# A two-layer hybrid decoder step on one core: sample transposes later, first-layer keys laid out by token tile, scans that start from the neighbouring block's column

## The chip, the cores and the metric

One core of a Trainium2 chip runs the whole step as one program. The metric is the device time of an execution in microseconds (us); the median of three runs stands for the kernel, and one further execution is profiled. The engines are PE (matrix products), PEld (its weight loads), DVE (vector), ACT (activations), POOL (GpSimd) and SP (which issues the DMAs here).

## The reference

One step over a prompt of 1024 tokens and 8 sample groups of 8 tokens (64 sample rows), width 1024, float32. Layer 0 is gated linear attention (GLA, 4 heads, key width 128, value width 256), layer 1 is stick-breaking attention (16 heads of 64). Both end in `x + (mixer(norm(x)) * silu(gate)) @ w_out`. Cut to what matters:

```python
# layer 0, per chunk of 64 tokens and per head; b is the running sum of the log decay
qd = qc * exp(b);  kd = kc * exp(-b)
att = where(causal, qd @ kd.T, 0)
o = qd @ s + att @ vc
s_new = s * exp(b_last)[:, None] + (kc * exp(b_last - b)).T @ vc

# layer 1, per head: key s is read by query t iff s < t
z = q @ k.T * dh ** -0.5 + bias
log_1mb = where(valid, log_sigmoid(-z), 0)
rest = cumsum(log_1mb, axis=3, reverse=True)
a = exp(where(valid, z + rest, -inf))
o = a @ v
```

The samples do the same, with a GLA state of their own (8 states per head) and, in layer 1, 256 keys and values from a paged cache before their own 8. Outputs are the new activations, the GLA states, and the keys and values of layer 1.

## The kernel before

Tokens are worked in tiles of 128: t = 0 to 7 are the prompt (NP = 8), t = 8 the 64 sample rows. Wide products are float32 split in a high and a low part (`whi`, `wlo`, `h0`, `h1`), three products for one: `dense` (L293) gives token rows, `dense_t` (L315) gives transposed columns, both into a bank `acc` of PSUM. PSUM is a pool with two banks per name (`acc`, `z`, `tr`, `o`): a third tile of a name waits until the first one's readers are done.

A time line written by hand sets the order of **PE**'s instructions: `at(time, function)` puts a step at a time whose unit is one dense tile, and steps are emitted in that order. The order of all other engines' queues is made by a scheduler that runs over the whole program; each engine then takes its own queue strictly in order and waits on semaphores.

**Layer 0.** For each head, three column stretches of queries and keys (`CH`) come from `dense_t`; `q_out` (L491) and `k_out` (L500) write five products into one tile `g` of 1536 columns: queries by exp(b) at 0, keys by exp(-b) at 384, keys by the decay to the tile's end at 768, and two half-tile products at 1152 and 1344. `gla_att` (L539) then makes a tile's scores `pat` with three products: all keys against the first 64 queries (L546), the first 64 keys against the last 64 queries (L547), the last 64 keys against the last 64 queries (L548), the last two into upper and lower partitions. Per head the sample states are read by `sample_out` (L610, product L615, two groups of states per call) and updated by `sample_state` (L620, product L625 into `z`, then DVE L628); both are called for b = 0, 2, 4, 6, at S_OUT + 0.05 b and S_STATE + 0.08 b after the head's last tile.

**Layer 1.** Heads go in 8 pairs. A pair's columns (384 per token tile) are made tile by tile, `columns(t)`, with gates after each second tile. For each tile DVE sums squares (`qk_sums`, L796), POOL raises them to the power -0.5 (L798) and DVE scales (`qk_scale`, L804), which frees the bank `acc`. Transposes on PE (L823) follow: `qk_p` for two prompt tiles, `qk_s` for the samples. The last column step of a pair is the samples' (t = NP), ending at time e; `qk_scale` of it is placed at e + C_SC (0.6), `qk_s` at e + C_T (0.9). The next pair's columns start at e.

Attention works in units: one head, 128 x 2 queries against 256 keys. `logits` (L875) puts scores in `z`, ACT makes `om` (1 - sigmoid) and `A` (L878, L879), POOL masks both when the unit is on the diagonal (L884). `stick` (L887) makes the running product from right to left with a DVE scan per half (L900) into `run`, 257 columns wide; column 256 holds what the block behind gives: 1 by a POOL memset (L894) on the diagonal, else a DVE copy of that block's column 0 (L896). The scan's first value is read from that column, and `A` is multiplied by `run` one column to the right (L905 diagonal, L908 else). `turn` (L910) transposes `A` on PE (L924), `weigh` (L936) multiplies by the values.

```python
    C_SC, C_T = 0.6, 0.9
    at(e + C_T, qk_s, st, p)
    at(z0 + L_STICK, stick, u, pair, m, c, j)
    at(z0 + L_TURN, turn, u, m, c)
```

Of the kernel before, what the change touches and what calls it, by code (L numbers as in the profile page):

```python
# [24 lines left out]
GH, DK, DV = 4, 128, 256  # L25
# [51 lines left out]
def tile_hybrid_decoder(ctx, tc, x_prompt, x_sample, state_gla, cache_k, cache_v, page_table,  # L77
# [3 lines left out]
    nc = tc.nc  # L81
# [24 lines left out]

    C_SC, C_T = 0.6, 0.9
    UNIT0, PACE, L_STICK, L_TURN, L_AV = 1.45, 0.42, 0.26, 0.8, 1.3
# [307 lines left out]
    for t in range(NP + 1):  # L416
        st = {}
# [73 lines left out]
    def q_out(st, h, c):  # L491
        n, nt = CH[c][1], (3, 3, 2)[c]

        g = st["g"] = sb("l0", "g", [128, 1536], F32, 3)
        nc.vector.scalar_tensor_tensor(g[:, :n], st["q"][:, :n], DK ** -0.5, st["e1"][:, :n],
                                       op0=OP.mult, op1=OP.mult)
        nc.vector.scalar_tensor_tensor(v3(g[:, 1152:], nt, 64), v3(st["q"], nt)[:, :, 64:], DK ** -0.5,
                                       st["e3"][:, :nt], op0=OP.mult, op1=OP.mult)

    def k_out(st, h, c):  # L500
        n, nt = CH[c][1], (3, 3, 2)[c]
        g = st["g"]
        nc.vector.tensor_mul(g[:, 384:384 + n], st["k"][:, :n], st["e2"][:, :n])
        nc.vector.tensor_mul(g[:, 768:768 + n], st["k"][:, :n], st["e4"][:, :n])
        nc.vector.tensor_mul(v3(g[:, 1344:], nt, 64), v3(st["k"], nt)[:, :, :64], st["e5"][:, :nt])

# [32 lines left out]
    def gla_att(st, t):  # L539
        g, o = st["g"], (t % 3) * 128  # L540
        pat = bank("z")
        att = st["att"] = sb("l0", "att", [128, 128], F32, 1)
        tr = psum.tile([128, 4, 128], F32, name="tr")
        if t < NP:
            o2 = 1344 + (t % 3) * 64
            nc.tensor.matmul(pat[:, :64], g[:, 384 + o:512 + o], g[:, o:o + 64], start=True, stop=True)  # L546
            nc.tensor.matmul(pat[:64, 64:128], g[:, o2:o2 + 64], g[:, o + 64:o + 128], start=True, stop=True)  # L547
            nc.tensor.matmul(pat[64:, 64:128], g[:, 448 + o:512 + o], g[:, o + 64:o + 128], start=True, stop=True)  # L548
            nc.vector.tensor_mul(att, pat[:, :128], C0["cmask"])
            split_att(st, 128)  # L550
            if t > 0:

                qh, ql = st["qs"] = [sb("l0", x, [128, 128], F32R, 1) for x in ("qh", "ql")]
                for x, y in ((slice(0, 64), o), (slice(64, 128), 1152 + (t % 3) * 64)):
                    nc.scalar.activation(qh[:, x], g[:, y:y + 64], AF.Copy)
                    nc.vector.tensor_sub(ql[:, x], g[:, y:y + 64], qh[:, x])
            nc.tensor.transpose(tr[:, 0, :], g[:, 768 + o:896 + o], ident)
            kh, kl = st["ks"] = [sb("l0", x, [128, 128], F32R, 1) for x in ("kh", "kl")]
            nc.scalar.activation(kh, tr[:, 0, :], AF.Copy)
            nc.vector.tensor_sub(kl, tr[:, 0, :], kh)  # L560
        else:
            nc.tensor.matmul(pat[:64, :64], g[:, 384 + o:448 + o], g[:, o:o + 64], start=True, stop=True)
            nc.vector.tensor_mul(att[:64, :64], pat[:64, :64], C0["smask"].rearrange("p b t -> p (b t)"))
            split_att(st, 64)
            nc.vector.tensor_copy(C0["qdm"].rearrange("p g (b s) -> p g b s", s=40)[:, :, :, :TS],
                                  g[:, o:o + 64].rearrange("p (g b s) -> p g b s", g=2, s=TS))
            nc.tensor.transpose(tr[:64, 0, :], g[:, 768 + o:832 + o], ident)

            kp = sb("l0", "kh", [128, 128], F32R, 1)
            nc.scalar.activation(kp[:64], tr[:64, 0, :], AF.Copy)  # L570
            nc.vector.tensor_sub(kp[64:], tr[:64, 0, :], kp[:64])
            ksm = st["ksm"] = sb("mid", "x4", [128, D + 1], F32R, 3)
            nc.vector.tensor_mul(ksm[:, :D].rearrange("p (b s) -> p b s", b=NB),
                                 kp[:, None].to_broadcast([128, NB, 128]),
                                 C0["blk2"][:, :, None].to_broadcast([128, NB, 128]))
# [80 lines left out]
    for h in range(GH):  # L656
# [24 lines left out]
        for t in range(NP + 1):  # L681
# [205 lines left out]
    def stick(u, pair, m, c, j):  # L887
# [93 lines left out]
    for p in range(PAIRS):  # L981
# [4 lines left out]
        def columns(t, i, span):  # L986
# [252 lines left out]
```

## Time and profile before

| | |
|---|---|
| three runs | 1405.91, 1409.91, 1410.98 us; median 1409.91 |
| profiled execution | 1409.71 us; its span 1407.7 us |
| granted TensorE clock, mean | 0.981 |
| PE / PEld busy | 1298.7 us (92%) / 1149.4 us (82%) |
| DVE, ACT, POOL busy | 1036.2 (74%), 710.7 (50%), 564.0 (40%) us |
| chain that ended last | PE 58%, DVE 20%, issue 8%, ACT 6%, POOL 5%, DMA 3% |
| DMA | 115.82 MB, mean 82 GB/s |

Layer 0 fills the span from 0 to about 445 us (some 95 us a head), its output product goes to about 538, layer 1's eight pairs follow at about 89 us each to 1251, and the samples' attention with the last output product ends it. A share of the span is an average over these; what a change is worth is read in its own stage. A wait is put down to the instruction that released it last. The view by stretch has, per row: the stretch, its length, the busy time of PE, PEld, DVE, ACT and POOL (x instructions) in it, the granted TensorE clock (1.00 is 2.4 GHz, 0.50 is 1.2 GHz), the DMA share and GB/s.

### The profile page before, as it was taken

What the parts mean: (1) busy time and instruction counts of PE and PEld (TensorE: products, weight loads), DVE (VectorE), ACT (ScalarE), POOL (GpSimd) and SP (SyncE); (2) the same over time, 40 slices, a digit from 0 to 9 for tenths busy, and PEclk for the clock granted to TensorE, in tenths of its full rate; (3) what the DMA queues carried; (4) which work ended last, traced back from release to release, by engine and by line L of the source; (5) the groups of instructions that cost most, each with busy time, mean ns of one, the idle gap of its engine ahead of it and who ended that gap; (6) DMA issues with size and microseconds to landing.
All of it is one profiled execution on the core that took longest, in us unless ns stands there. A gap on an engine that the chain in (4) does not pass through costs nothing.

```text
span 1407.7 us, 23743 instructions
## 1 busy us (share of the span) xinstructions
PE 1298.7 (92%) x8089; PEld 1149.4 (82%) x8089; DVE 1036.2 (74%) x2139; ACT 710.7 (50%) x1640; POOL 564.0 (40%) x1005
## 2 busy tenths in 40 slices
PE   6999999999999998989889898998998989889998
PEld 5788887888877788879889898897987988877666
DVE  7848648558464357688888888888888898897453
ACT  6445145253451034566756666566665666663221
POOL 6223314224131206464545645546464564542000
PEclk9999999999999999999999999999999999999999
DMA  7311402304336433020110201102012022133772
GB/s 190 90 31 42 133 15 70 106 22 120 102 115 223 128 105 108 19 76 22 56 41 20 77 17 48 53 24 75 18 37 63 22 80 62 41 113 116 266 254 90
DMA packets 118458, 115.82 MB, mean 82 GB/s; under 512 B 11002, under 2 KB 97922, under 8 KB 118338
## 3 DMA queue, kind: packets, MB, share of 16 engines
q1 hardware_dynamic: 118338, 114.31, 26.5%
q8 instruction: 64, 1.05, 0.3%
q14 instruction: 56, 0.46, 0.1%
HBM read 83.61 MB, written 30.67 MB: 81 GB/s over the span
## 4 chain that ended last, share of the span: by engine, by line
PE 58%; DVE 20%; issue 8%; ACT 6%; POOL 5%; DMA 3%; SPq 0%; POOLq 0%; DVEq 0%; ACTq 0%
PE acc L293 34%; PE acc L315 7%; DVE run L900 5%; PE z L875 3%; PE tr L924 3%; PE o L936 2%; DVE A L908 2%; ACT qh L847 2%; DVE A L905 1%; POOL rs L798 1%; PE o L537 1%; DVE whi L221 1%; DVE aT L927 1%; PE tr L277 1%; POOL wlo L222 1%
## 5 line engine op out<-in xcount | busy, mean ns | idle before, releaser
L293 PE MATMUL acc<-whi,h 128*128 128x512 f32 (+1 forms) x1728 | 548.0, 380 | 14.1 <-DVE qk L804 13.5
L293 PEld LDWEIGHTS acc<-whi,h 128*128 128x128 f32 x1728 | 320.3, 193 | 45.6 <-ACT gt L860 12.3
L293 PE MATMUL acc<-wlo,h 128*128 128x512 f32 (+1 forms) x864 | 326.7, 378 | 3.9 <-DVE wlo L222 2.5
L900 DVE TENSOR_TENSOR_SCAN run<-om,run 128x256 f32<-128x256 f32 (+1 forms) x320 | 231.5, 762 | 6.7 <-POOL om L884 4.2
L315 PE MATMUL acc<-h,whi 128*128 128x256 f32 (+5 forms) x832 | 191.8, 315 | 5.2 <-ACT h L282 2.9
L222 POOL TENSOR_TENSOR wlo<-wr,whi 128x512 fp32r<-128x512 f32 x98 | 139.4, 1427 | 140.9 <-DVE whi L221 111.6
L293 PEld LDWEIGHTS acc<-wlo,h 128*128 128x128 f32 x864 | 165.9, 192 | 23.2 <-DVE wlo L222 3.2
L926 ACT ACTIVATE aT<-tr 128x512 fp32r<-128x512 f32 (+1 forms) x160 | 88.9, 555 | 122.4 <-PE tr L924 117.3
L315 PEld LDWEIGHTS acc<-h,whi 128*128 128x128 f32 (+2 forms) x832 | 139.2, 186 | 10.1 <-issue 5.0
L878 ACT ACTIVATE om<-z,bias 128x512 f32<-128x512 f32 (+1 forms) x160 | 103.1, 645 | 51.2 <-PE z L875 32.7
L293 PE MATMUL acc<-w,h 128*128 128x384 f32 (+1 forms) x480 | 126.7, 375 | 1.8 <-DVE qk L804 1.8
L798 POOL TENSOR_TENSOR rs<-ms,half_exp 128x4 f32<-128x4 f32 (+1 forms) x72 | 95.3, 1323 | 79.6 <-DVE ms L796 79.3
L927 DVE TENSOR_TENSOR aT<-tr,aT 128x512 fp32r<-128x512 f32 (+1 forms) x160 | 100.8, 630 | 33.1 <-ACT aT L926 31.0
L315 PE MATMUL acc<-h,wlo 128*128 128x256 f32 (+2 forms) x392 | 122.9, 314 | 0.7 <-POOL wlo L222 0.7
L924 PE MATMUL tr<-ident,A 128*128 128x128 f32 x576 | 93.4, 282 | 28.2 <-DVE kc L853 21.2
L924 PEld LDWEIGHTS tr<-ident,A 128*128 128x128 f32 x576 | 72.0, 145 | 42.8 <-issue 24.5
L936 PE MATMUL o<-aT,v 128*128 128x256 f32 x640 | 102.3, 282 | 0.0
L879 ACT ACTIVATE A<-z,bias 128x512 f32<-128x512 f32 (+1 forms) x160 | 102.2, 639 | 0.0
L936 PEld LDWEIGHTS o<-aT,v 128*128 128x128 f32 x640 | 95.8, 190 | 0.7
L875 PE MATMUL z<-kc,qh 128*128 128x256 f32 x320 | 85.6, 289 | 7.3 <-DVE kc L852 7.3
L293 PEld LDWEIGHTS acc<-w,h 128*128 128x128 f32 x480 | 85.3, 195 | 8.5 <-issue 2.5
L875 PE MATMUL z<-kc,ql 128*128 128x256 f32 x320 | 84.6, 286 | 0.0
(274 smaller groups left out, 2444.0 us busy)
## 6 DMA issues: line engine op xcount, KB each, us to landing
wr<-in_w_in_b_dram SPq DMA_DIRECT2D x64, 256.0 KB, 3.0
wr<-in_w_in_a_dram SPq DMA_DIRECT2D x32, 256.0 KB, 2.7
kp<-in_cache_k_dram SPq DMA_DIRECT2D x16, 512.0 KB, 5.3
vp<-in_cache_v_dram SPq DMA_DIRECT2D x16, 512.0 KB, 4.7
o_d<-og SPq DMA_DIRECT2D x60, 128.0 KB, 1.8
x<-in_x_prompt_dram SPq DMA_DIRECT2D x8, 512.0 KB, 5.0
wr<-in_w_in_a_dram SPq DMA_DIRECT2D x32, 128.0 KB, 3.0
n<-in_state_gla_dram SPq DMA_DIRECT2D x8, 512.0 KB, 3.9
```

Source lines behind the costliest of these rows:

```text
L222: engine.tensor_sub(e.lo[:, :m], raw[:, :m], e.hi[:, :m])
L293: nc.tensor.matmul(st["ps"][:x.shape[1], :n], x, (w[k].hi if part == 0 else w[k].lo)[:, :n], start=first, stop=last)
L315: nc.tensor.matmul(st[key][:x.shape[1], :n], x, y, start=first, stop=last)
L798: nc.gpsimd.tensor_tensor(st["rs"][:n], ms[:n], half_exp[:n], op=OP.pow)
L875: nc.tensor.matmul(out, lhs, rhs, start=x == 0, stop=x == len(mm) - 1)
L878: nc.scalar.activation(u["om"][:, v0:], z[:, v0:], AF.Sigmoid, scale=-1.0, bias=K1["bias"][:, 1, hd:hd + 1])
L879: nc.scalar.activation(u["A"][:, v0:], z[:, v0:], AF.Sigmoid, bias=K1["bias"][:, 0, hd:hd + 1])
L900: nc.vector.tensor_tensor_scan(run[:, a, n - 1::-1], rev, rev, run[:, a, n:n + 1], op0=OP.mult, op1=OP.bypass)
L924: nc.tensor.transpose(tr[:, x], u["A"][:, col:col + 128], ident)
L926: nc.scalar.activation(hi[:, v0:], tr[:, v0:], AF.Copy)
L927: nc.vector.tensor_sub(lo[:, v0:], tr[:, v0:], hi[:, v0:])
L936: nc.tensor.matmul(q["po"][:, j], vs, part[:, x * 256:(x + 1) * 256], start=first and n == 0, stop=last and n == 3)
```

## The change

Four parts. (1) `qk_s` moves from e + 0.9 to e + 2.1 (C_TS). (2) The keys by exp(-b) and by the half-tile decay are written interleaved by token tile, 64 columns each: first half by exp(-b), first half by the half-tile decay, second half by exp(-b). The last 64 queries then meet 128 neighbouring columns in one product, so that a tile has two products of 128 x 64 where it had three; the quarter that is not causal is masked as before. The samples' keys get a small multiply of their own. (3) All `sample_out` calls of a head stand at one time, and `sample_state` calls stand 0.13 b apart instead of 0.08 b. (4) A scan takes its first value straight from the block behind (`before[:, a, 0:1]`, or 1.0 on the diagonal); the copy of that column, which the multiply still needs, goes from DVE to POOL.

```diff
-    C_SC, C_T = 0.6, 0.9
+    C_SC, C_T, C_TS = 0.6, 0.9, 2.1
...
     def k_out(st, h, c):
-        nc.vector.tensor_mul(g[:, 384:384 + n], st["k"][:, :n], st["e2"][:, :n])
-        nc.vector.tensor_mul(g[:, 768:768 + n], st["k"][:, :n], st["e4"][:, :n])
-        nc.vector.tensor_mul(v3(g[:, 1344:], nt, 64), v3(st["k"], nt)[:, :, :64], st["e5"][:, :nt])
+        def halves(x):
+            return x[:, :nt * 128].rearrange("p (c a s) -> p c a s", a=2, s=64)
+        by_tile = g[:, 384:384 + nt * 192].rearrange("p (c a s) -> p c a s", a=3, s=64)
+        nc.vector.tensor_mul(by_tile[:, :, 0::2], halves(st["k"]), halves(st["e2"]))
+        if c == 2:
+            nc.vector.tensor_mul(g[:, 768:832], st["k"][:, 256:320], st["e2"][:, 256:320])
+        nc.vector.tensor_mul(g[:, 960:960 + n], st["k"][:, :n], st["e4"][:, :n])
+        nc.vector.tensor_mul(by_tile[:, :, 1], v3(st["k"], nt)[:, :, :64], st["e5"][:, :nt])
...
     def gla_att(st, t):
-            nc.tensor.matmul(pat[:, :64], g[:, 384 + o:512 + o], g[:, o:o + 64], start=True, stop=True)
-            nc.tensor.matmul(pat[:64, 64:128], g[:, o2:o2 + 64], g[:, o + 64:o + 128], start=True, stop=True)
-            nc.tensor.matmul(pat[64:, 64:128], g[:, 448 + o:512 + o], g[:, o + 64:o + 128], start=True, stop=True)
+            nc.tensor.matmul(pat[:, :64], g[:, kt:kt + 128], g[:, o:o + 64], start=True, stop=True)
+            nc.tensor.matmul(pat[:, 64:128], g[:, kt + 64:kt + 192], g[:, o + 64:o + 128], start=True, stop=True)
...
-                    at(i + S_OUT + 0.05 * b, sample_out, st, b)
-                    at(i + S_STATE + 0.08 * b, sample_state, st, h, b)
+                    at(i + S_OUT + 0.2, sample_out, st, b)
+                    at(i + S_STATE + 0.13 * b, sample_state, st, h, b)
...
-    at(i + 2.2, closed, "l0")
+    at(i + 2.5, closed, "l0")
...
     def stick(u, pair, m, c, j):
-            nc.vector.tensor_copy(run[:, :, 256:], before[:, :, 0:1])
+            nc.gpsimd.tensor_copy(run[:, :, 256:], before[:, :, 0:1])
         for a in range(2):
             n = ends[a]
+            init = 1.0 if diag else before[:, a, 0:1]
-            nc.vector.tensor_tensor_scan(run[:, a, n - 1::-1], rev, rev, run[:, a, n:n + 1],
+            nc.vector.tensor_tensor_scan(run[:, a, n - 1::-1], rev, rev, init,
                                          op0=OP.mult, op1=OP.bypass)
...
-                at(e + C_T, qk_s, st, p)
+                at(e + C_TS, qk_s, st, p)
```

How this moves the queues, in three places. The line numbers of the changed kernel differ by some lines, a scan is printed as SCALAR_TENSOR_TENSOR, and [waits X_49] names the engines whose semaphores an instruction waits for.

**PE, between the second pair and the third.** Before, the sample transposes (L823, `qk 128x64`) stand inside the next pair's second column step:

```order
L936 MATMUL o<-aT_7949,v_7404 128x256 [waits Activation_49,Pool_49]
L936 MATMUL o<-aT_7950,v_7404 128x256 [waits DVE_49,Pool_49]
L936 MATMUL o<-aT_7949,v_7404 128x256
L936 MATMUL o<-aT_7950,v_7404 128x256
L293 MATMUL acc<-wlo,h_80 128x384
L823 MATMUL tr<-ident,qk 128x64 [waits DVE_49,PE_49]
L823 MATMUL tr<-ident,qk 128x64
L293 MATMUL acc<-whi,h_81 128x384
L293 MATMUL acc<-whi,h_80 128x384
L293 MATMUL acc<-wlo,h_80 128x384
L293 MATMUL acc<-whi,h_81 128x384
```

In the change (there L829) they stand behind that pair's first gates, some 65 rows of PE's queue later:

```order
L315 MATMUL acc<-h_80,w_7799 128x256
L293 MATMUL acc<-whi,h_80 128x384 [waits DVE_49,PE_49,Activation_49]
L293 MATMUL acc<-wlo,h_80 128x384
L932 MATMUL tr<-ident,A 128x128 x4
L293 MATMUL acc<-whi,h_81 128x384
L829 MATMUL tr<-ident,qk 128x64 [waits PE_49]
L829 MATMUL tr<-ident,qk 128x64
L881 MATMUL z<-kc,qh 128x256
L881 MATMUL z<-kc,ql_5787 128x256
```

The wait for DVE that stood on them is gone from them; the products behind them no longer follow them.

**DVE, the first two units of the third pair.** Before, the copy (L896) stands between a unit's multiplies (L905) and the next unit's scans (L900), and the scan waits for it:

```order
L900 SCALAR_TENSOR_TENSOR run<-om,run 128x128 [waits Pool_49]
L900 SCALAR_TENSOR_TENSOR run<-om,run 128x256
L905 TENSOR_TENSOR A<-A,run 128x128 [waits DVE_49,Pool_49]
L905 TENSOR_TENSOR A<-A,run 128x256 [waits DVE_49]
L896 COPY run<-run 128x2
L796 TENSOR_REDUCE ms_8095<-sq 128x4 [waits Activation_49]
L900 SCALAR_TENSOR_TENSOR run<-om,run 128x256 [waits DVE_49]
L900 SCALAR_TENSOR_TENSOR run<-om,run 128x256
```

In the change (scans L908, multiplies L913 and L916) no copy stands there, the next unit's first scan comes between the two diagonal multiplies, and the later multiply waits for POOL:

```order
L908 SCALAR_TENSOR_TENSOR run<-om 128x128 [waits Pool_49]
L908 SCALAR_TENSOR_TENSOR run<-om 128x256
L913 TENSOR_TENSOR A<-A,run 128x128 [waits DVE_49,Pool_49]
L908 SCALAR_TENSOR_TENSOR run<-om,run 128x256 [waits Activation_49]
L913 TENSOR_TENSOR A<-A,run 128x256 [waits DVE_49]
L908 SCALAR_TENSOR_TENSOR run<-om,run 128x256
L802 TENSOR_REDUCE ms_8062<-sq 128x4 [waits Activation_49]
L916 TENSOR_TENSOR A<-A,run 128x512 [waits DVE_49,Pool_49]
```

**POOL, at the end of the second pair.** Before, the subtractions that make `wlo` (L222) stand together, ahead of the power for the samples (L798, `ms 64x4`):

```order
L222 TENSOR_TENSOR w_7827<-wr,w_7826 128x512 [waits PE_49,Activation_49]
L918 MEMSET aT_7949 128x128 [waits DVE_49,PE_49]
L222 TENSOR_TENSOR w_7835<-wr,w_7834 128x512 [waits DMAHW6_49,Activation_49]
L918 MEMSET aT_7950 128x128 [waits PE_49]
L222 TENSOR_TENSOR w_7860<-wr,w_7859 128x512 [waits DMAHW7_49,Activation_49]
L222 TENSOR_TENSOR wlo<-wr,whi 128x512 [waits DMAHW0_49,Activation_49]
L894 MEMSET run 128x1 [waits DVE_49]
L894 MEMSET run 128x1
L798 TENSOR_TENSOR rs_7926<-ms_7921,half_exp 64x4 [waits DVE_49]
```

In the change the copies (L903) stand among them, each waiting for a scan of DVE, and the memset of `run` (L900) has gone behind the power (L804):

```order
L222 TENSOR_TENSOR w_7799<-wr,w_7798 128x512 [waits PE_49,Activation_49]
L903 COPY run<-run 128x2 [waits DVE_49]
L926 MEMSET aT_7921 128x128 [waits PE_49]
L222 TENSOR_TENSOR w_7807<-wr,w_7806 128x512 [waits DMAHW6_49,Activation_49]
L926 MEMSET aT_7922 128x128 [waits PE_49]
L222 TENSOR_TENSOR w_7832<-wr,w_7831 128x512 [waits DMAHW7_49,Activation_49]
L903 COPY run<-run 128x2 [waits DVE_49,Pool_49]
L222 TENSOR_TENSOR wlo<-wr,whi 128x512 [waits DMAHW0_49,Activation_49]
L804 TENSOR_TENSOR rs_7898<-ms_7893,half_exp 64x4 [waits DVE_49]
L900 MEMSET run 128x1 [waits DVE_49,Pool_49]
```

## Rows read from the trace of the kernel before

**Rows 1.** Busy time of the engines by stretch: us, then busy us (x instructions) per engine
```profile
160.00:255.00 95.00, 92.14 (x518) 78.16 (x517) 64.02 (x162) 39.39 (x122) 27.84 (x35) 1.00 0.23 67
...
709.90:800.50 90.60, 83.14 (x554) 80.35 (x555) 77.31 (x153) 57.79 (x122) 49.51 (x95) 0.95 0.14 42
...
889.80:979.30 89.50, 80.43 (x554) 77.43 (x555) 77.25 (x153) 57.69 (x122) 48.93 (x95) 0.98 0.15 43
```

**Rows 2.** Who PE waited for, whole span: us in total, times, longest us
```profile
PE tr L924 <- DVE kc L853: 21.2, 8, 2.9
...
PE tr L823 <- DVE qk L804: 21.2, 8, 3.4
...
PE acc L293 <- DVE qk L804: 15.2, 11, 2.4
...
PE z L625 <- DVE n L628: 8.1, 3, 2.8
```

**Rows 3.** Timeline of PE, 700 to 735: start us, us, what, [idle before <- releaser]
```profile
709.91 0.45 PE L823 MATMUL tr<-ident,qk 64*128 64x64 f32 x2 [3.33 <-DVE qk L804]
...
718.61 0.49 PE L924 MATMUL tr<-ident,A 128*128 128x128 f32 x3
```

**Rows 4.** The view of rows 1, around two boundaries between head pairs; PEclk is the granted clock
```profile
620.40:624.00 3.60, 3.60 (x13) 3.44 (x14) 1.14 (x4) 0.00 (x0) 3.60 (x7) 0.53 0.32 85
...
706.00:709.90 3.90, 0.57 (x5) 0.34 (x4) 3.80 (x5) 1.81 (x4) 3.63 (x4) 0.93 0.06 17
...
714.00:716.00 2.00, 2.00 (x11) 2.00 (x10) 0.57 (x1) 0.63 (x2) 0.00 (x0) 0.50 0.45 132
```

**Rows 5.** Timeline of POOL (as rows 3), 684 to 716
```profile
701.09 1.29 POOL L222 TENSOR_TENSOR wlo<-wr,whi 128x512 fp32r<-128x512 f32 x1
...
704.50 0.13 POOL L894 MEMSET run<- 128x1 f32 x2 [2.12 <-DVE run L896]
...
705.30 2.02 POOL L798 TENSOR_TENSOR rs<-ms,half_exp 64x4 f32<-64x4 f32 x1 [0.67 <-DVE ms L796]
...
707.30 1.25 POOL L222 TENSOR_TENSOR wlo<-wr,whi 128x512 fp32r<-128x512 f32 x1
...
712.25 0.40 POOL L884 TENSOR_SCALAR_AFFINE_SELECT om<-om 128x256 f32<-128x256 f32 x1
```

**Rows 6.** Timeline of DVE (as rows 3), two windows of 652 to 731
```profile
665.86 0.70 DVE L896 COPY run<-run 128x2 f32<-128x2 f32 x1
...
696.12 1.22 DVE L896 COPY run<-run 128x2 f32<-128x2 f32 x1
...
701.71 1.86 DVE L900 TENSOR_TENSOR_SCAN run<-om,run 128x256 f32<-128x256 f32 x2
...
706.62 2.48 DVE L908 TENSOR_TENSOR A<-A,run 128x512 f32<-128x512 f32 x1
...
716.04 1.11 DVE L900 TENSOR_TENSOR_SCAN run<-om,run 128x128 f32<-128x128 f32 x2
...
717.07 0.60 DVE L905 TENSOR_TENSOR A<-A,run 128x128 f32<-128x128 f32 x2
```

**Rows 7.** Groups of DVE: busy us, mean ns; tile run on POOL: ns min/median/max
```profile
L896 DVE COPY run<-run 128x2 f32<-128x2 f32 x96 | 26.0, 271 | 0.2
...
L894 POOL MEMSET run<- x16: 93/98/99, 633.4 to 704.5; 128x1 f32 x16
```

**Rows 8.** Timeline of PE at 149, and the view of rows 1
```profile
149.15 0.38 PE L625 MATMUL z<-vh,x 128*128 128x256 f32 x1 [2.57 <-DVE n L628]
...
149.60:153.00 3.40, 3.40 (x15) 3.40 (x14) 2.68 (x7) 0.00 (x0) 1.25 (x1) 0.50 0.53 161
```

**Rows 9.** Timeline of PE in layer 0 (as rows 3), 203 to 212
```profile
209.51 0.33 PE L546 MATMUL z<-g 128*128 128x64 f32 x2
...
209.78 0.27 PE L547 MATMUL z<-g 128*64 128x64 f32 x1
...
210.04 0.33 PE L557 MATMUL tr<-ident,g 128*128 128x128 f32 x1
```

More of the change, by code (lines that the diff above doesn't have):

```diff
@@ L496, in q_out @@
                                        op0=OP.mult, op1=OP.mult)
-        nc.vector.scalar_tensor_tensor(v3(g[:, 1152:], nt, 64), v3(st["q"], nt)[:, :, 64:], DK ** -0.5,
+        nc.vector.scalar_tensor_tensor(v3(g[:, 1344:], nt, 64), v3(st["q"], nt)[:, :, 64:], DK ** -0.5,
                                        st["e3"][:, :nt], op0=OP.mult, op1=OP.mult)
@@ L539, in gla_att @@
     def gla_att(st, t):
-        g, o = st["g"], (t % 3) * 128
+        g, o, kt = st["g"], (t % 3) * 128, 384 + (t % 3) * 192
         pat = bank("z")
@@ L544, in gla_att @@
         if t < NP:
-            o2 = 1344 + (t % 3) * 64
-            nc.tensor.matmul(pat[:, :64], g[:, 384 + o:512 + o], g[:, o:o + 64], start=True, stop=True)
-            nc.tensor.matmul(pat[:64, 64:128], g[:, o2:o2 + 64], g[:, o + 64:o + 128], start=True, stop=True)
-            nc.tensor.matmul(pat[64:, 64:128], g[:, 448 + o:512 + o], g[:, o + 64:o + 128], start=True, stop=True)
+            nc.tensor.matmul(pat[:, :64], g[:, kt:kt + 128], g[:, o:o + 64], start=True, stop=True)
+            nc.tensor.matmul(pat[:, 64:128], g[:, kt + 64:kt + 192], g[:, o + 64:o + 128], start=True, stop=True)
             nc.vector.tensor_mul(att, pat[:, :128], C0["cmask"])
@@ L553, in gla_att @@
                 qh, ql = st["qs"] = [sb("l0", x, [128, 128], F32R, 1) for x in ("qh", "ql")]
-                for x, y in ((slice(0, 64), o), (slice(64, 128), 1152 + (t % 3) * 64)):
+                for x, y in ((slice(0, 64), o), (slice(64, 128), 1344 + (t % 3) * 64)):
                     nc.scalar.activation(qh[:, x], g[:, y:y + 64], AF.Copy)
                     nc.vector.tensor_sub(ql[:, x], g[:, y:y + 64], qh[:, x])
-            nc.tensor.transpose(tr[:, 0, :], g[:, 768 + o:896 + o], ident)
+            nc.tensor.transpose(tr[:, 0, :], g[:, 960 + o:1088 + o], ident)
             kh, kl = st["ks"] = [sb("l0", x, [128, 128], F32R, 1) for x in ("kh", "kl")]
@@ L561, in gla_att @@
         else:
-            nc.tensor.matmul(pat[:64, :64], g[:, 384 + o:448 + o], g[:, o:o + 64], start=True, stop=True)
+            nc.tensor.matmul(pat[:64, :64], g[:, kt:kt + 64], g[:, o:o + 64], start=True, stop=True)
             nc.vector.tensor_mul(att[:64, :64], pat[:64, :64], C0["smask"].rearrange("p b t -> p (b t)"))
@@ L566, in gla_att @@
                                   g[:, o:o + 64].rearrange("p (g b s) -> p g b s", g=2, s=TS))
-            nc.tensor.transpose(tr[:64, 0, :], g[:, 768 + o:832 + o], ident)
+            nc.tensor.transpose(tr[:64, 0, :], g[:, 960 + o:1024 + o], ident)
             kp = sb("l0", "kh", [128, 128], F32R, 1)
```

## The prediction

> **What bounds it now.** I read the busy time by stretch first [rows 1]. In layer 0 (one head, 160 to 255 us) PE is busy 92.1 of 95.0 us and DVE 64.0. In a pair of layer 1 (889.8 to 979.3) PE has 80.4 of 89.5, DVE 77.3 and POOL 48.9. PE sets the end in both, but in a pair DVE is nearly as full, so time won on PE there can soon be time waited for DVE. Then the list of PE's waits [rows 2]. Four lines matter: PE stood 8 times, once per pair, for `qk_scale` before the sample transposes (L823), 21.2 us in all; 8 times before a unit's transposes for `kc` (L853), 21.2; 15.2 for `qk_scale` before a column product; and 3 times, 8.1, in layer 0 for DVE's state updates (L628). The timeline of PE [rows 3] shows where: between the second and third pair it stands 3.33 us until 709.91. The clock is the second half of that price [rows 4]: PE was busy 0.57 of the 3.9 us from 706, and by 714 to 716 the granted clock is 0.50, its lower level (1.2 GHz); after the boundary before it 3.6 us average 0.53. The engines behind these waits are POOL [rows 5] and DVE [rows 6], whose short work between is in [rows 7].
>
> The sum is made against the profiled execution, 1409.71 us, 0.2 under the median of the runs. About 0.5% (7 us) can be told from no change.
>
> **Sample transposes (A).** The move takes away eight waits of 21.2 us. Behind them lie 1.7 us lost to the clock where 3.6 us ran at 0.53 (3.6 x 0.47), and 3.0 where 6 us ran at 0.50 [rows 4]; I take 2.2 a pair, 18 in all. So 39 us are there, 4.9 a pair, if nothing else makes PE wait. But something is late next. After the step PE needs, inside the next pair's first gates, the transposes of that pair's first diagonal unit, at 718.61 today [rows 3]. Their `A` comes from this chain: POOL's queue (power 2.02 from 705.30, subtraction 1.25 from 707.30, and so on to the mask of `om`, 0.40 from 712.25) [rows 5], then two scans, 1.11, and two multiplies, 0.60 [rows 6]. In the new queue of DVE one scan of the next unit stands between these multiplies, 0.93 by half of the 1.86 that two took at 701.71 [rows 6]. That gives 712.65 + 1.11 + 0.60 + 0.93 = 715.3. PE can come 3.3 us earlier to this place, not the 6.3 (3.33 + 3.0) that the step and the clock would free; it would stand about 3 us here. A stand of that length was followed by the low clock, which costs 1.7 to 3.0 again. I take a gain of 2.0 a pair (3.3, less 1.3 because PE waits once more for the second tile's `qk_scale` anyway, which hides part of a slow clock): 16 us. The ends: 0.3 a pair (3.3 - 3.0), 2 us; and 39. Nothing waits for the later `qTs` and `kTs` but the samples' attention, after all pairs; the sample `qk` buffer is held longer, one of four, which the queues don't show as a wait. The queue that the step passes on PE is all work of the next pair; it issues no DMA.
>
> **Copies to POOL (B).** DVE loses 96 copies, 26.0 us busy, mean 0.271 [rows 7]. Most are short, so what counts is two of them in a pair: the one of 1.22 at 696.12, in the unbroken work of DVE that ends in the `kc` wait, and the one of 0.70 at 665.86, ahead of the squares, power and `qk_scale` that end a wait of the third line [rows 2, 6]. I take 0.7 of the first and 0.4 of the second in 8 pairs, 9 us. The ends are nothing and (1.22 + 0.70) x 8 = 15.
>
> On POOL a copy has no row. The nearest are a memset of one column, 0.098 [rows 7], and the mask of 128 x 256, 0.40 [rows 5]; I take 0.2, since it reads as well as writes: 19 us more on an engine that is idle 40 of 89.5 us in a pair. The new wait matters more. At the boundary POOL reached a `wlo` subtraction at 701.09; now a copy stands before it and waits for two scans that ended at 703.57 (701.71 + 1.86) [rows 5, 6]. Behind it are that subtraction, the samples' power and all that leads to the mask. POOL stood idle 2.12 us before 704.50 and 0.67 before 705.30 [rows 5], which just covers the 2.5; those weights are used a pair later. If the cover is gone, the mask comes later by as much (third rival). The multiply that now waits for the copy comes after two scans of its own, which take longer than the copy. I charge nothing.
>
> What row and rule say of DVE and POOL side by side: the multiply at 706.62 took 2.48 us and the copy at 696.12 took 1.22, both while POOL worked on a power or a subtraction [rows 5, 6], so the two engines do hold each other up. The Trainium skill, page "SBUF — State Buffer", section "Who interferes with whom", has it that DVE with two inputs in SBUF and a GpSimd instruction that reads SBUF lock each other out, whole instruction against whole instruction. That speaks against this part: scans and multiplies have two such inputs, and a copy on POOL reads SBUF where the memset did not. By the rule the sum would lose B; by the rows I keep it, since both ends of that are in the range.
>
> **Keys by token tile (C).** In layer 0 the first product starts at 209.51, the two half-width ones at 209.78 and the tile's transpose at 210.04 [rows 9]: 0.26 each, with the two half-width ones together taking no more than one. So counting one matmul fewer would mislead. One wide product takes the place of the pair: it costs the same 0.26, or as little as nothing if it runs on behind its like. I take the middle, 0.13 x 32 tiles = 4 us (ends 0 and 8.3), all on PE, which is full there. The Trainium skill, page "TensorEngine Tiling (Array Packing)", "Key Properties", says that a change of tiling mode drains the array; by it the upper end is nearer, as two changes a tile go. Four extra multiplies of 64 columns on DVE lie beside a DVE that is idle 31 of 95 us [rows 1]; without that cover they would cost under 0.6 each, 2.4.
>
> **Sample states (D).** The third state product stood 2.57 at 149.15 [rows 8], 8.1 for three heads [rows 2]. It now comes ten products of a dense tile later, and in DVE's queue the two query products that stood between are ahead of the weights' scaling. I take 6.5 of the 8.1. The low clock from 149.60 to 153.00 (0.50, 3.4 us) [rows 8] lost 1.7; I take 1.5. Twelve changes between narrow and wide products go with the bunched `sample_out`; no row prices one, between nothing and 0.26 each; I take 1 us in all. D is 9, ends 4 and 13. If DVE is still late, its wait stays; nothing else is queued that PE needs.
>
> **Sum.** 16 + 9 + 4 + 9 = 38: 1409.7 - 38 = **1372 us**. All lower ends give 6 (1404), all upper ends 75 (1335).
>
> **Rivals.**
> 1. *Nothing is late next.* A pays its 39: 1372 - 23 = 1349. For it: DVE is busy 0.57 of the 2 us from 714 today [rows 4], so it has room there to catch up. Against: POOL's queue, which does not depend on PE's step. Chance 0.15.
> 2. *The wait moves whole.* DVE and POOL keep a pair at 89.5; A and B give nothing, C and D stay: 1409.7 - 13 = 1397. For it: a pair at a mean clock of 0.95 takes 90.6 us and one at 0.98 takes 89.5 [rows 1], so PE's own speed hardly sets a pair's length; and DVE's 77.3 of 89.5. Against: DVE loses its copies. Chance 0.20.
> 3. *Slower: POOL's queue becomes the bound.* The copies' waits for scans hold back the power and the mask at each boundary. The mask may come 3.3 us later than 712.65 before PE is later than today (715.3 + 3.3 = 718.6); beyond that every us counts. Two copies that each hold it 2.5 give 5.0, so 1.7 too late, and a fresh low clock 1.7: 3.4 x 7 boundaries = 24, less C and D, 13: 1421. Against: POOL's idle 2.8 us there. Chance 0.07.
> 4. *Copies and scans hold each other up*, as the 2.48 and the 1.22 show for other work [rows 6]: each copy on POOL costs DVE about the 0.27 that it did, B is 0: 1381. For it: scans run right behind one another when a copy comes due. Against: the copy is short. Chance 0.15. This is what the page on SBUF states as a rule (Trainium skill, section above).
> 5. *It does not do what it says.* The wait moves whole and DVE is still late for the states, so only C is left: 1406. Chance 0.08.
>
> **How the numbers follow.** My forecast has 0.35, with its own range 1360 to 1385. The range 1341 to 1401 takes in rivals 2 and 4 and most of rival 1; it leaves out 3, 5 and a little of 1, under 0.2. Faster by over 0.5%: the forecast and rivals 1, 2 and 4, 0.85. Same: rival 5, 0.08. Slower: rival 3, 0.07.
>
> **What would show it.** A right: no wait before the sample transposes in the list, and in its place one of 2 to 4 us a pair before the first diagonal unit's transposes or the first gates; pairs of 86 to 87 us. B right: the `kc` wait under 2 us; the copy on POOL at 0.1 to 0.4; no multiply of DVE that a POOL copy released. C: two products of 128 x 64 within 0.53 us. D: L628's line gone from the list, clock 1.00 at 150. Wrong: pairs still of 89 us (rival 2), masks on POOL later within the pair (3), scans stretched beside copies (4).

## The result and the profile after

The changed kernel takes 1372.12 us (median of 4 runs, 1370.72 to 1375.27) against 1410.45 for the kernel before beside it: ratio 0.9736, 95% interval 0.9707 to 0.9765. The forecast was 1372. Below, a saving is worked out as (1 - ratio) x 1409.7, and what separates two kernels as the difference of their ratios. An interval is some 0.0025 either way, so such a difference carries about 5 us; where the medians give another figure, both stand.

The profiled execution has a span of 1373.6 us and a mean clock of 0.986 (before 0.981). In its timeline of PE the first product on the samples' columns of the last head stands at 396.5 us (before 410.6), the one of the last pair at 1197.0 (before 1231.6). So layer 0 gave 14.1 us and the way from there to the last pair another 20.5, of which 18.0 fall to the seven pairs (by their samples' columns); what follows gave nothing (176.6 us after 176.1). This execution was the longest of the four, so these shares may be some 3 us low. The list of PE's waits, whole span (us in total, times, longest):

```profile
PE tr L932 <- POOL v L819: 18.3, 6, 3.1
PE tr L932 <- DVE kc L859: 11.9, 8, 1.8
PE acc L293 <- DVE qk L810: 8.6, 10, 1.7
...
PE acc L315 <- DVE g L512: 5.1, 3, 1.7
```

Against [rows 2]: the wait of the sample transposes (21.2) and the one for the state updates (8.1) are gone, the `kc` wait fell from 21.2 to 11.9 and the `qk` wait from 15.2 to 8.6. Two lines are new. The first is a stand before the transposes of the next pair's first diagonal unit, six times 3.03 to 3.07 us; the other is a wait in layer 0, once in each of three heads. The busy time by stretch (columns as in [rows 1]):

```profile
160.00:255.00 95.00, 93.04 (x520) 81.10 (x519) 67.54 (x168) 41.08 (x127) 26.65 (x36) 1.00 0.27 77
...
759.10:846.20 87.10, 80.55 (x556) 77.46 (x555) 73.70 (x141) 57.48 (x122) 53.30 (x107) 0.98 0.15 44
...
784.90:788.30 3.40, 3.40 (x19) 3.40 (x18) 3.29 (x7) 1.65 (x3) 2.51 (x4) 0.50 0.00 0
...
149.60:153.00 3.40, 3.40 (x26) 3.40 (x25) 3.30 (x9) 0.00 (x0) 0.00 (x0) 1.00 0.65 150
```

This pair takes 87.1 us where two before took 89.5 and 90.6 [rows 1]. In it DVE lost 3.6 us (77.3 to 73.7), POOL gained 4. It is the shortest: from one pair's samples' columns to the next the seven take 87.1 to 88.6, 87.7 on average, where they took 89.3 to 92.9, 90.2 on average. The third row is what follows the new stand: the clock falls to 0.50 there as it did before. The last row, at the place of [rows 8], now has 1.00.

What the new stand waits for is read from three timelines. POOL at the boundary:

```profile
774.02 1.38 POOL L804 TENSOR_TENSOR rs<-ms,half_exp 64x4 f32<-64x4 f32 x1
...
775.51 1.71 POOL L222 TENSOR_TENSOR wlo<-wr,whi 128x512 fp32r<-128x512 f32 x1
...
777.62 1.01 POOL L804 TENSOR_TENSOR rs<-ms,half_exp 128x4 f32<-128x4 f32 x1
...
779.00 1.28 POOL L222 TENSOR_TENSOR w<-wr,w 128x512 fp32r<-128x512 f32 x1
780.24 0.41 POOL L890 TENSOR_SCALAR_AFFINE_SELECT om<-om 128x256 f32<-128x256 f32 x1
...
783.17 0.53 POOL L819 CAST v<-v 128x128 fp32r<-128x128 f32 x1
```

ACT and DVE beside it:

```profile
775.09 0.59 ACT L884 ACTIVATE om<-z,bias 128x384 f32<-128x384 f32 x1
...
780.68 1.47 DVE L908 TENSOR_TENSOR_SCAN run<-om 128x128 f32<-128x128 f32 x2 [1.01 <-POOL om L890]
782.08 0.47 DVE L913 TENSOR_TENSOR A<-A,run 128x128 f32<-128x128 f32 x1
782.47 0.77 DVE L908 TENSOR_TENSOR_SCAN run<-om,run 128x256 f32<-128x256 f32 x1
783.17 0.39 DVE L913 TENSOR_TENSOR A<-A,run 128x256 f32<-128x256 f32 x1
```

And PE:

```profile
783.71 0.52 PE L932 MATMUL tr<-ident,A 128*128 128x128 f32 x3 [3.07 <-POOL v L819]
```

`om` was there at 775.68 (775.09 + 0.59); its mask starts 4.6 us later, behind a power (777.62), two weight subtractions that nobody needs before the next pair, and small work. DVE stood 1.01 us for it. Then come scans, a multiply, a scan of the next unit, and the second multiply, which ends at 783.56; PE starts 0.15 later. The list names POOL's cast of `v` because that ended at 783.70; it is the multiply that PE waits for, as the runs with other timing below show.

### The profile page after: what moved, and what is told of

It is laid out like the page before. It is cut to its first block, busy times and chain, and to the rows that moved or that the text cites. A ratio compares the mean times of both kernels' runs of the same rounds, so it can differ in the third digit from the quotient of the medians.

```text
span 1373.6 us, 23656 instructions
## 1 busy us (share of the span) xinstructions
PE 1282.8 (93%) x8025; PEld 1140.3 (83%) x8025; DVE 1012.5 (74%) x2047; ACT 709.7 (52%) x1640; POOL 587.0 (43%) x1101
## 4 chain that ended last, share of the span: by engine, by line
PE 55%; DVE 18%; POOL 9%; ACT 7%; issue 7%; DMA 3%; SPq 1%; POOLq 0%; ACTq 0%; DVEq 0%
PE acc L293 31%; PE acc L315 7%; DVE run L908 4%; PE z L881 3%; PE tr L932 3%; PE o L944 2%; POOL wlo L222 2%; POOL rs L804 2%; ACT qh L853 2%; DVE whi L221 2%; PE o L544 1%; DVE aT L935 1%; DVE wr L217 1%; POOL v L819 1%; PE o L1154 1%
## 5 line engine op out<-in xcount | busy, mean ns | idle before, releaser
L293 PE MATMUL acc<-whi,h 128*128 128x512 f32 (+1 forms) x1728 | 538.7, 374 | 10.1 <-DVE qk L810 7.9
L293 PEld LDWEIGHTS acc<-whi,h 128*128 128x128 f32 x1728 | 313.5, 189 | 41.1 <-ACT sh L954 4.2
L293 PE MATMUL acc<-wlo,h 128*128 128x512 f32 (+1 forms) x864 | 322.5, 373 | 3.9 <-DVE wlo L222 2.5
L222 POOL TENSOR_TENSOR wlo<-wr,whi 128x512 fp32r<-128x512 f32 x98 | 139.1, 1422 | 123.5 <-DVE whi L221 93.2
L293 PEld LDWEIGHTS acc<-wlo,h 128*128 128x128 f32 x864 | 162.8, 188 | 22.7 <-DVE wlo L222 3.2
L908 DVE TENSOR_TENSOR_SCAN run<-om,run 128x256 f32<-128x256 f32 x192 | 146.7, 802 | 11.0 <-ACT om L884 10.5
L934 ACT ACTIVATE aT<-tr 128x512 fp32r<-128x512 f32 (+1 forms) x160 | 88.9, 556 | 103.9 <-PE tr L932 90.2
L293 PE MATMUL acc<-w,h 128*128 128x384 f32 (+1 forms) x480 | 122.6, 365 | 0.7 <-DVE qk L810 0.7
L908 DVE TENSOR_TENSOR_SCAN run<-om 128x128 f32<-128x128 f32 (+1 forms) x128 | 85.0, 695 | 13.6 <-POOL om L890 13.6
L804 POOL TENSOR_TENSOR rs<-ms,half_exp 128x4 f32<-128x4 f32 (+1 forms) x72 | 83.9, 1166 | 20.3 <-DVE ms L802 18.8
L293 PEld LDWEIGHTS acc<-w,h 128*128 128x128 f32 x480 | 82.2, 189 | 7.2 <-issue 2.5
```

The lines of the kernel that those rows point to most:

```text
L222: engine.tensor_sub(e.lo[:, :m], raw[:, :m], e.hi[:, :m])
L293: nc.tensor.matmul(st["ps"][:x.shape[1], :n], x, (w[k].hi if part == 0 else w[k].lo)[:, :n], start=first, stop=last)
L804: nc.gpsimd.tensor_tensor(st["rs"][:n], ms[:n], half_exp[:n], op=OP.pow)
L934: nc.scalar.activation(hi[:, v0:], tr[:, v0:], AF.Copy)
```

## The experiments

**The four parts one by one**, each put alone into the kernel before.

The sample transposes (A):

```diff
-                at(e + C_T, qk_s, st, p)
+                at(e + C_TS, qk_s, st, p)
```

> The kernel before with the later sample transposes alone. Theory (the forecast's term A): the eight waits for qk_scale before the sample transposes go, but a stand of about 3 us comes in their place before each next pair's first diagonal unit's transposes, so 16 us faster, ratio 0.989. Rival 'nothing late next': no such stand, 39 us faster, 0.972. Rival 'the two parts need each other': without the copies taken off DVE, DVE is late all the same, and the wait moves whole: under 4 us, 0.997 to 1.0.

Measured: 1398.79 us, ratio 0.9918 [0.9891, 0.9946], 11.6 us. The forecast's mechanism, a size smaller. Two rows of its timeline of PE at one boundary:

```profile
882.19 0.63 PE L924 MATMUL tr<-ident,A 128*128 128x128 f32 x4 [0.98 <-DVE A L908]
...
888.00 0.52 PE L924 MATMUL tr<-ident,A 128*128 128x128 f32 x3 [1.82 <-POOL v L813]
```

The sample transposes' wait is gone and two waits stand in its place, 2.8 us here and 13.8 in all where 21.2 went. The low clock did not come back behind them here: from 888 to 892 it is 1.00.

The copies on POOL and the scans' own start (B):

```diff
-            nc.vector.tensor_copy(run[:, :, 256:], before[:, :, 0:1])
+            nc.gpsimd.tensor_copy(run[:, :, 256:], before[:, :, 0:1])
...
-            nc.vector.tensor_tensor_scan(run[:, a, n - 1::-1], rev, rev, run[:, a, n:n + 1],
+            nc.vector.tensor_tensor_scan(run[:, a, n - 1::-1], rev, rev, init,
```

> The kernel before with the column copies on POOL and the scans that take their first value from the block behind, alone. Theory (term B): the kc wait falls from 2.6 to about 1.4 us a pair and the qk wait by 0.4, 9 us faster, 0.994; the wait before the sample transposes stays, since it hangs on POOL's power and DVE's squares. Rival 'copies and scans hold each other up': 0 us, 1.0, with scans or multiplies of DVE longer by some 0.27 us a unit. Rival 'POOL's queue': the copies stand in it before the sample power, and the sample transposes' wait grows by up to 2.5 us a pair: up to 20 us slower, 1.014.

Measured: 1386.97 us, 0.9843 [0.9810, 0.9876], 22.1 us, more than twice the forecast's term and the largest part. From its list of waits:

```profile
PE tr L823 <- DVE qk L804: 18.9, 8, 2.7
PE tr L926 <- DVE kc L853: 11.9, 8, 1.9
...
PE acc L293 <- DVE qk L804: 7.0, 10, 1.3
```

Against [rows 2], `kc` lost 9.3 us and the `qk` wait 8.2, where I had 0.7 and 0.4 a pair (8.8). The sample transposes still stand 18.9.

The keys by token tile (C), the hunks of `q_out`, `k_out` and `gla_att`, in the main:

```diff
-            nc.tensor.matmul(pat[:64, 64:128], g[:, o2:o2 + 64], g[:, o + 64:o + 128], start=True, stop=True)
-            nc.tensor.matmul(pat[64:, 64:128], g[:, 448 + o:512 + o], g[:, o + 64:o + 128], start=True, stop=True)
+            nc.tensor.matmul(pat[:, 64:128], g[:, kt + 64:kt + 192], g[:, o + 64:o + 128], start=True, stop=True)
```

> The kernel before with layer 0's keys by token tile alone (one product of 128 x 64 for two half-width ones). Theory (term C): 4 us faster, 0.997, all in layer 0. Rival 'free': the half-width pair cost no more than the wide one, 0 us. Rival 'drains': each tile saves 0.26, 8.3 us, 0.994. Rival 'DVE': the wait for the last tile's query product on DVE, 1.7 us in each of three heads of the changed kernel, comes from the extra multiplies in k_out; then it shows here too and the gain is 5 us less.

Measured: 1405.70 us, 0.9971 [0.9953, 0.9988], 4.1 us, as the forecast had it, but not for its reason. The wait for the state updates stays, and in two heads that had a full clock the low one now follows it: its list of waits (L631 is the state product), then one such stretch.

```profile
PE z L631 <- DVE n L634: 8.4, 3, 2.9
```

```profile
243.50:246.90 3.40, 3.05 (x11) 3.05 (x12) 2.80 (x8) 0.00 (x0) 1.27 (x1) 0.51 0.48 159
```

Two more such stretches take back 3.4 x 0.5 x 2 = 3.4 us. The 1.7 us wait of the changed kernel does not show here.

The sample states (D):

```diff
-                    at(i + S_OUT + 0.05 * b, sample_out, st, b)
-                    at(i + S_STATE + 0.08 * b, sample_state, st, h, b)
+                    at(i + S_OUT + 0.2, sample_out, st, b)
+                    at(i + S_STATE + 0.13 * b, sample_state, st, h, b)
```

> The kernel before with the bunched sample outputs and the later, wider spaced sample states alone. Theory (term D): the waits for the state updates (2.6 to 2.9 us in each of three heads) go, and the low clock behind each: 9 us faster, 0.994; layer 1 unchanged. Rival: if the 1.7 us wait for the last query product that the changed kernel shows in layer 0 comes with this part, 4 us faster, 0.997. Upper end 13 us, 0.991, if bunching costs nothing.

Measured: 1403.34 us, 0.9955 [0.9935, 0.9974], 6.3 us. The state wait is gone from its list and the new one is there:

```profile
PE acc L315 <- DVE g L505: 5.1, 3, 1.7
```

So the new wait of layer 0 belongs to D: 8.1 us of waits went, 5.1 came.

**A part taken out of the whole.** The singles add to 44.1 us, the change gives 37.2. Each of these three is the changed kernel with one part undone. The copy back on DVE, the scans' start as changed:

```diff
-            nc.gpsimd.tensor_copy(run[:, :, 256:], before[:, :, 0:1])
+            nc.vector.tensor_copy(run[:, :, 256:], before[:, :, 0:1])
```

> The changed kernel with the column copy back on DVE; the scans still take their first value from the block behind. Theory (it is the engine that counts): DVE does 96 copies again, the kc and qk waits go back to 2.6 and 1.75 us a pair, pairs to 88 us or more; the time becomes that of the later transposes alone (11.6 us) and layer 0's 15: about 1383, ratio to the kernel before 0.981. Rival (it is the scans' own start that counts): the time stays at 1372 to 1375, 0.973 to 0.975.

Measured: 1383.80 us, 0.9803 [0.9778, 0.9828]. Undone, the engine costs 0.0067, 9.4 us (11.7 by the medians). From its list of waits:

```profile
PE tr L932 <- DVE A L913: 22.9, 7, 4.1
PE tr L932 <- DVE kc L859: 20.1, 8, 2.9
PE acc L293 <- DVE qk L810: 9.1, 10, 1.6
```

The `kc` line is where it was, so that wait hangs on the engine of the copy. The `qk` line, which I expected back as well, stays at 9.1 (16.9 with A alone, 8.6 in the changed kernel): as far as these runs show, it hangs on the scans' own start. The stand before the diagonal transposes grew to 4.1.

The sample transposes at their old place:

```diff
-                at(e + C_TS, qk_s, st, p)
+                at(e + C_T, qk_s, st, p)
```

> The changed kernel with the sample transposes back at their old place. Theory (both parts shorten the same waits, and with the copies on POOL the later transposes only move a 2.7 us stand to a 3.1 us one): pairs stay at 87.5 us, 1372 plus or minus 4, ratio 0.971 to 0.976. Rival (each adds its own, as the forecast's sum has it): 11.6 to 16 us slower than the changed kernel, 1384 to 1388, 0.982 to 0.985.

Measured: 1373.33 us, 0.9723 [0.9697, 0.9749], no different from the changed kernel. With the copies on POOL, part A gives nothing:

```profile
868.20 0.31 PE L829 MATMUL tr<-ident,qk 64*128 64x64 f32 x2 [2.68 <-DVE qk L810]
```

A stand of 2.68 us here against one of 3.06 some rows later, and the low clock behind either (0.59 from 868.5 to 872).

The keys as before:

```diff
-            nc.tensor.matmul(pat[:, 64:128], g[:, kt + 64:kt + 192], g[:, o + 64:o + 128], start=True, stop=True)
+            nc.tensor.matmul(pat[:64, 64:128], g[:, o2:o2 + 64], g[:, o + 64:o + 128], start=True, stop=True)
+            nc.tensor.matmul(pat[64:, 64:128], g[:, 448 + o:512 + o], g[:, o + 64:o + 128], start=True, stop=True)
```

> The changed kernel with layer 0's keys as before (two half-width products). Theory (alone, the wide product gave only 0.9 us a head since DVE's state updates, on which PE waited, did not come earlier; with that wait gone it gives all of PE's saving): heads go from 92.0 back to the 93.9 of the run with the state part alone, 7.6 us slower than the changed kernel, 1380, ratio 0.979. Rival (its own 4.1 us, whatever else is there): 1376, 0.976.

Measured: 1380.87 us, 0.9804 [0.9778, 0.9830]; undone, C costs 0.0068, 9.6 us (8.8 by the medians), about twice what it gave alone. The intervals of the two overlap (4 to 15 here, 2 to 7 alone), so the traces must decide. One head by stretch, without C:

```profile
212.80:306.90 94.10, 91.85 (x520) 78.89 (x519) 66.78 (x163) 39.46 (x124) 25.91 (x35) 1.00 0.24 70
```

and in the changed kernel:

```profile
208.60:300.60 92.00, 90.04 (x504) 78.56 (x503) 66.09 (x164) 39.59 (x124) 26.03 (x35) 1.00 0.25 72
```

16 instructions of PE fewer, 1.8 us less busy, 2.1 us shorter, both at full clock. The samples' columns of the last head say the same: C alone brings them 2.2 us forward, D alone 5.3, both together 12.5 to 14.1 in the six runs that have both and nothing else new in layer 0.

**POOL's queue at the boundary.** The subtraction at 779.00, done twice on POOL:

```diff
         engine.tensor_sub(e.lo[:, :m], raw[:, :m], e.hi[:, :m])
+        if e.first > ACT_FROM and n % 8 == 5:
+            engine.tensor_sub(e.lo[:, :m], raw[:, :m], e.hi[:, :m])
```

> The changed kernel, in which POOL does one weight subtraction twice per pair, the one just ahead of the mask of om at the boundary (1.28 us). Theory (POOL's queue up to that mask sets the 3.1 us stand before the first diagonal transposes): each boundary 1.28 us longer, 7 of them 9 us, 1381, ratio 0.980, the stand 4.3 us. Rival (another engine or PE's own pace sets it): no change, 0.973.

Measured: 1381.81 us, 0.9788 [0.9764, 0.9811]: 9.7 us longer by the medians, 7.3 by the ratios. The size is the theory's, the way is not. The stand (line numbers are two higher here; the added subtraction is L224) is now put to the multiply:

```profile
878.14 0.52 PE L934 MATMUL tr<-ident,A 128*128 128x128 f32 x3 [4.58 <-DVE A L915]
```

POOL and DVE ahead of it:

```profile
873.16 0.40 POOL L892 TENSOR_SCALAR_AFFINE_SELECT om<-om 128x256 f32<-128x256 f32 x1
...
875.57 1.25 POOL L224 TENSOR_TENSOR wlo<-wr,whi 128x512 fp32r<-128x512 f32 x1
```

```profile
874.99 1.98 DVE L915 TENSOR_TENSOR A<-A,run 128x128 f32<-128x128 f32 x1
```

The scheduler put the second subtraction 2.4 us behind the start of the mask, not ahead of it. The mask comes no later: 21.2 to 21.3 us after the pair's samples' columns, as in the changed kernel (21.2 to 21.4). What grew is DVE's first diagonal multiply, 1.98 us beside that subtraction where it took 0.47, at all six boundaries. So this run says nothing of the queue ahead of the mask, and its agreement with the theory's 9 us is luck.

The same subtraction on DVE:

```diff
-            at(s, split, n, pool, nc.vector if n % 3 == 2 and DLO < e.first < ACT_FROM else nc.gpsimd)
+            at(s, split, n, pool, nc.vector if (n % 3 == 2 and DLO < e.first < ACT_FROM) or (e.first > ACT_FROM and n % 8 == 5) else nc.gpsimd)
```

> The changed kernel with that same subtraction on DVE in place of POOL, one a pair. Theory: the mask comes 1.25 us earlier and DVE, idle 1.0 us before its scan, does the subtraction (about 0.7 us) there; the stand shrinks by 0.3 to 1.0 us, 2 to 7 us in all: 1365 to 1370, ratio 0.968 to 0.972. Rival (DVE's queue is what counts): 0.7 us a pair slower, 5 us, 0.977.

Measured: 1362.25 us, 0.9654 [0.9631, 0.9678], 11.6 us less than the changed kernel (9.9 by the medians), more than the theory had. The stand fell by 1.2 us at six boundaries, as the mask came 1.0 us earlier (20.1 to 20.6 us after the samples' columns), and the low clock went at five of the six. The mask and PE's timeline one boundary later, then the stretch behind the same boundary as above (there the stand was 1.89) and the one behind the first boundary (stand 1.88), where the clock still fell:

```profile
862.07 0.40 POOL L890 TENSOR_SCALAR_AFFINE_SELECT om<-om 128x256 f32<-128x256 f32 x1
...
865.34 0.52 PE L932 MATMUL tr<-ident,A 128*128 128x128 f32 x3 [1.90 <-DVE A L913]
```

```profile
780.70:784.10 3.40, 2.57 (x22) 2.40 (x21) 3.40 (x8) 2.13 (x5) 2.64 (x5) 1.00 0.00 0
...
608.60:611.60 3.00, 3.00 (x16) 3.00 (x15) 2.76 (x7) 1.86 (x4) 2.06 (x3) 0.50 0.01 3
```

The mean clock of this run is 0.997.

This kernel with the sample transposes at their old place:

```diff
-                at(e + C_TS, qk_s, st, p)
+                at(e + C_T, qk_s, st, p)
```

> The kernel of e8 (one subtraction a pair on DVE) with the sample transposes back at their old place. Theory (the later transposes gain only once the mask comes early enough; at the old place PE stands for the samples' qk_scale, which the moved subtraction does not bring forward): a stand of about 2.6 us a pair, pairs of 87.5 us, the time of the changed kernel, 1372, ratio 0.973. Rival (the later transposes are worth nothing, it is all POOL's queue): 1362, 0.966.

Measured: 1367.54 us, 0.9717 [0.9689, 0.9745], between the two, nearer the theory. The transposes stand 2.67 us again:

```profile
862.57 0.45 PE L829 MATMUL tr<-ident,qk 64*128 64x64 f32 x2 [2.67 <-DVE qk L810]
```

So A, worth nothing in the changed kernel, is worth 0.0063, 8.9 us (5.3 by the medians), once the mask comes earlier.

**Layer 0's new wait.** One weight subtraction a head of layer 0 goes to DVE as well:

```diff
-nc.vector if (n % 3 == 2 and DLO < e.first < ACT_FROM)
+nc.vector if ((n % 3 == 2 or n > 12 and n % 12 == 6) and DLO < e.first < ACT_FROM)
```

> The kernel of e8 with one weight subtraction more per head of layer 0 on DVE in place of POOL: the one that runs on POOL from 136.25 us in the changed kernel. Theory (the new 1.7 us wait in layer 0 comes from POOL's subtraction holding up DVE's 128 x 64 subtraction ql, which took 1.84 us there and 0.22 elsewhere): ql is 0.2 again, DVE pays 0.67 for the moved one, so the wait falls from 1.7 to about 0.7 us in three heads, 3 us faster than e8, ratio to the kernel before 0.963. Rival (DVE is simply too full there): 0.67 us a head slower, 0.967.

In the changed kernel the timeline of DVE and POOL has this ahead of the wait, and the view of that line (count, ns min/median/max) this of all 56:

```profile
135.78 1.97 DVE L562 TENSOR_TENSOR ql<-g,qh 128x64 fp32r<-128x64 f32 x2
...
136.25 1.28 POOL L222 TENSOR_TENSOR wlo<-wr,whi 128x512 fp32r<-128x512 f32 x1
```

```profile
L562 DVE TENSOR_TENSOR ql<-g,qh x56: 201/218/1843, 38.7 to 397.2; 128x64 fp32r<-128x64 f32 x56
```

With the subtraction on DVE, the timeline of DVE, PE and POOL:

```profile
135.99 0.35 DVE L562 TENSOR_TENSOR ql<-g,qh 128x64 fp32r<-128x64 f32 x2
...
140.18 0.62 PE L315 MATMUL acc<-h,whi 128*128 128x384 f32 x2 [0.82 <-DVE g L512]
...
140.59 4.13 POOL L222 TENSOR_TENSOR wlo<-wr,whi 128x512 fp32r<-128x512 f32 x1 [2.57 <-DVE whi L221]
```

Measured: 1360.66 us, 0.9657 [0.9631, 0.9682]. The mechanism holds, the pair of `ql` subtractions takes 0.35 and the wait 0.82, but the time is that of e8 within the noise. A head's length hardly moved (91.7 us after 92.0, by the samples' column products). Of the 0.9 us a head, 0.5 went into PE itself, busy 90.5 us after 90.0 with as many instructions; why stays open.

**A second subtraction a pair on DVE**, the one at 775.51:

```diff
-(e.first > ACT_FROM and n % 8 == 5)
+(e.first > ACT_FROM and n % 8 in (4, 5))
```

> The kernel of e9 with a second subtraction per pair on DVE (the one before the samples' v in POOL's queue, 1.71 us). Theory: the mask comes up to 1.7 us earlier on POOL, but DVE has only 0.6 us idle left in e8 there and must do 0.67 more, so between 3 us faster and 3 us slower than e9, ratio 0.961 to 0.965; the stand before the first diagonal transposes goes under 1.9 us. Rival (POOL alone sets it): the stand goes to 0.3, 1.6 us a pair, 11 us faster than e9, 0.955.

Measured: 1349.68 us, 0.9586 [0.9559, 0.9613]: 10.0 us under e9 by the ratios, 11.0 by the medians, the rival's size. My theory that DVE was full there is wrong. The mask, PE's stand at a boundary, and a pair by stretch:

```profile
856.55 0.64 POOL L890 TENSOR_SCALAR_AFFINE_SELECT om<-om 128x256 f32<-128x256 f32 x1
...
859.58 0.52 PE L932 MATMUL tr<-ident,A 128*128 128x128 f32 x3 [0.71 <-DVE A L913]
```

```profile
837.40:922.00 84.60, 79.13 (x556) 76.00 (x556) 74.11 (x143) 57.44 (x122) 51.33 (x105) 1.00 0.16 46
```

The pair has 84.6 us at full clock, and DVE in it no more busy time than in e8 (74.3 us). With the changed kernel and e8 this makes three places of the mask, at some 21.3, 20.2 and 19.2 us after the samples' columns; PE's diagonal transposes follow at 24.8, 23.5 and 22.3. That is what shows the queue ahead of the mask to set the stand. This kernel is the fastest of the study, 4.1% under the kernel before and 1.5% under the changed one (0.9586 / 0.9736).

## Why the prediction was right, and where its steps were not

The time was right to 0.1 us, and the terms by layer nearly: 25 for layer 1 (measured 20.5), 13 for layer 0 (14.1 by the timelines). Three of the four terms were not, and so close a sum is luck. Alone the parts give 11.6, 22.1, 4.1 and 6.3; in the change A and B share one saving while C and D help each other, and these errors cancel.

- **A, 16 us.** The mechanism was right for the change: the wait goes, and PE stands about 3 us (3.03 to 3.07) before the first diagonal transposes, because POOL's queue, then the mask, two scans, a multiply, the next unit's scan and a multiply come first; e8 and e11 show that it is that queue. The low clock came back as foretold (not with A alone). What failed is the step "I take a gain of 2.0 a pair" as a term of its own: alone A gave 11.6, in the change nothing (e6). With B in, the wait at the old place is 2.67 us and the one that A puts in its place 3.06. It is B, too, that brings the mask forward, from 22.7 to 21.2 us after the samples' columns; A alone leaves it at 22.7.
- **B, 9 us.** Mis-sized: 22.1 alone. I priced two copies a pair at 0.7 and 0.4; the two waits fell by 1.2 (2.62 to 1.44) and 1.1 (1.75 to 0.65), and the sample transposes' wait went from 21.2 us [rows 2] to 18.9 in all. On top of A, the engine of the copy alone is worth 9.4 (e5), by chance just the term; the scans' own start was not taken out by itself. The copy on POOL was taken at 0.2: the median is 0.188 us, the mean 0.285. The new wait of the multiply cost nothing, as charged. Rival 4 fell as a price on the copies: the scans beside them take 0.80 us on average where they took 0.79, and the non-diagonal multiply, which went up to 2.50 us before, takes 0.764 at most now. That the two engines hold each other up in longer work is still so (e7).
- **C, 4 us.** Alone 4.1, but in the change 9.6. The step "I take the middle" failed; the upper end of 8.3 was nearer, and alone the low clock behind the state wait took back 3.4 us (e3). The Trainium skill, page "TensorEngine Tiling (Array Packing)", section "Key Properties", has a change of tiling mode drain the array, which spoke for the upper end; e12's 1.8 us of PE busy time a head, 0.23 a tile, agrees with that end, 0.26.
- **D, 9 us.** 6.3 alone. The wait and the low clock went as foretold (clock 1.00 at 150). The step "nothing else is queued that PE needs" failed: with PE on time, the next columns' product waits 1.7 us for `k_out` on DVE; with POOL's subtraction moved it is 0.8 (e9), so about half of it came from there. The change as a whole did not show this as a loss, since C pays more with D than without.

Rivals: *nothing late next* (1349) is about the time that e11 reaches, where POOL's queue is relieved; *the wait moves whole* is true of A alone once B is there. *POOL's queue* as a loss did not come: the copies keep POOL busy for 27.3 us, but with them the mask comes 1.5 us earlier, not later. Even so that queue became what PE stands for at a boundary.

## What to carry to other kernels

When two edits shorten waits that end at the same place, price them together against what is late next, not one by one: here one was worth 12 us alone, nothing beside the other, and 5 to 9 again when the next limit moved. Look in the queue of an engine that is less than half busy for work with no due date in front of work on the critical path; moving two of POOL's weight subtractions a pair gave some 21 us more, in two steps of about 10. And look where a scheduler put an added instruction before reading its cost: the one of e7 cost what was expected, but by holding up another engine.

## What was not expected of the hardware

A 128 x 64 subtraction on DVE took 1.84 us beside a subtraction on POOL of 1.28 us, and 0.22 at the median. In e7 a multiply on DVE took 1.98 beside one of 1.25, and 0.47 without it. In e9 it went the other way: POOL's subtraction took 4.13 us from 140.59 while DVE ran two scans, a subtraction and multiplies. The DVE subtraction of 1.84 us ended at 137.75, 0.2 us after POOL's, as if it had waited for its end; the multiply of e7 ended 0.15 after. The Trainium skill, page "SBUF — State Buffer", section "Who interferes with whom", states such an exclusive lock between the two, and these rows agree; the small copies, which the same rule would have made dear, were not.

The clock: in the changed kernel the granted clock was 0.50 for 3.4 us behind a stand of 3.07 us; in e8, behind one of 1.9 us at the same place, it stayed at 1.00. Behind the first boundary of e8 a stand of 1.88 was followed by 0.50 all the same, so the length of a stand does not decide it alone. Over six boundaries 1.2 us less of stand make 7; e8 won 11.6 (9.9 by the medians), and the low clock that went at five of them is the likely rest.
